# Transforms in plain float32 and an output projection placed among the long convolutions, in a two-block model kernel

## The chip, the cores and the metric

The kernel runs on one core of one Trainium2 chip. The metric is the time of one execution on the device, in microseconds (us), as the median of the runs shown. The engines are named as in the profile: PE is TensorE (PEld its weight loads), DVE is VectorE, ACT is ScalarE, POOL is GpSimd, SP is SyncE, which issues the DMAs.

## The reference, cut to what matters

Two blocks follow each other on a sequence of 512 positions and 1024 features. The change is in the mixing part of the first: a gated recurrence (branch a) and two long convolutions (branch b) read the same normalised input, and their projected outputs are gated and added. The rest of the first block is a mixture of 16 experts; the second block is two layers of attention and a feed-forward part.

```python
proj = h @ w_in[l]
a_x, a_gate, hy, gates = jnp.split(proj, ...)
xa = dwconv(a_x, conv_a_w[l], conv_a_b[l], ...)
h_a = rg_lru(xa, ..., False) + rg_lru(xa, ..., True)
y_a = (h_a * jax.nn.gelu(a_gate)) @ w_a_out[l]
hy = dwconv(hy, conv_b_w[l], conv_b_b[l], ...)
v, x1, x2 = jnp.split(hy, 3, axis=-1)
filt = hyena_filters(S, ...)
z = v
for n, gate in enumerate((x1, x2)):
    k = bidir_kernel(filt[:, n, 0], filt[:, n, 1])
    z = gate * fftconv(z, k, filt_bias[l, n])     # rfft, product, irfft
y_b = z @ w_b_out[l]
g_a, g_b = jnp.split(jax.nn.sigmoid(gates), 2, axis=-1)
x = x + (g_a * y_a + g_b * y_b) @ w_o[l]
```

## The kernel before

Activations lie with features on the 128 partitions and the 512 positions along a row: eight tiles of 128x512 make the 1024 features (`c.x`). A projection onto 128 output features (`proj`, line 952) takes a 128x1024 weight tile from HBM, splits it into a rounded float32r part and the rest (`split`, lines 152 and 155: a cast on ACT, a subtraction on DVE), and multiplies each of its eight 128x128 pieces with the two parts of an activation tile, which was split in the same way. `mm3` (lines 163 to 165) does this in three passes, hi x hi, hi x lo and lo x hi; 24 matmuls of 512 columns make one projection.

`body_t1` runs the stages of the first block's mixing part:

- **Norm and gelu gate** (lines 969 to 1009): eight projections whose gelu ends in `c.x`. `filter_mlp` (1073) loads the transform matrix, splits it into `dft_h` and `dft_l` (1075 to 1079) and makes the filters' hidden layer `HS`.
- **recurrence** (1112): the order is the string `STEPS_A`. A step `i` projects and convolves a tile of input, `r` runs the recurrence on it and multiplies the result into `c.x`, `f` makes a group of 256 filters (1253: a matmul, a product with the decay, a split into `sdh` and `sdl`), `t` transforms it (1291) and stores it in HBM (`c.kd`), `G` computes one of the 16 gate tiles (959) and stores it in HBM (`c.gates`).
- **branch_a** (1183): splits the eight tiles of `c.x` into `yah` and `yal`, then does eight projections with `w_a`; each loads its gate tile, forms (gate + 1) x result on DVE (1196) and stores it in HBM (`c.mg`).
- **branch_b** (1301): the order is the string `STEPS_B`. A step `c` projects and convolves one tile of v, x1 or x2 (24 in all; the digits are the group of 256 features, which of the three, and which half). `u` transposes a pair of tiles on PE into an operand of a transform (split into `uh`, `ul`, line 1335) or into a gate (1347). `L` is a long convolution (1364): forward transform, product with a stored filter spectrum (1354), combinations, a split into `Yh` and `Yl` (1385 to 1390). `M` is the inverse transform (1392) and the gating: `gated` (1404) makes the split operand of the second convolution, `last` (1417) transposes back and writes to `c.x`. `G` steps project the remaining six gates.
- **Merge** (1038 to 1069): splits `c.x`, projects with `w_b`, adds the tiles of `c.mg`, projects with `w_o`.

A transform is folded into products of 128x128 matrices with 256 columns (`part`, 1213, two products in one PSUM tile; `pair`, 1220, two such tiles whose sum and difference DVE forms). A filter transform has 12 products, a forward one 8, an inverse one 8. Each product is an `mm3`.

The strings set the order in which the steps are written. The framework then orders each engine's instructions by what is ready and earlier in the text, and adds the waits; in the timeline, matmuls of a transform stand between those of a projection. Tiles come from pools with a number of buffers for each name (`CFG1`: `U` 3, `cv` 9, `Y` 4 and so on), and a step waits where no buffer is free. PSUM gives three tiles to the projections, three to forward transforms and two to transposes and inverse transforms. All loads and stores are issued by SP, in one queue.

Of the kernel before, what the change touches and what calls it, by code (L numbers as in the profile page):

```python
# [844 lines left out]
STEPS_A = "i0 G8 i1 r0 f0 t0 i2 f2 r1 t2 f1 t1 i3 f3 r2 i4 G1 r3 i5 G0 r4 G2 i6 t3 r5 f4 t4 G4 f5 t5 f6 G7 i7 r6 t6 f7 G3 G5 r7 Gb t7 G6"  # L845
STEPS_B = "c000 c001 c020 c010 c120 c200 c011 u00 c100 c101 u01 L00 c201 M00 c110 u10 u20 c220 L01 c111 u11 L10 c021 c121 M01 M10 L11 c300 M11 c301 c320 L20 c210 c211 c321 c310 u21 u30 M20 c311 L21 L30 Gf u31 c221 M21 M30 Ga L31 M31 Ge Gc G9 Gd"
CFG1 = dict(acc=3, c=2, f=3, hA=0, lA=1, gh=0, gl=1, hB=0, lB=1, kh=0, kl=1, xh=0, xl=1, sh=0, sl=1, yh=0, yl=1, wl=1, rA=1, rX=1, bl=0, tA=5, tB=5, cv=9, U=3, Y=4, th=5, fA='vvvv', fB='vvvv', gB='vvvv', hB2='vvvv', xg=1, K=1, zh=0, zl=1)
ACTDVE, POOLDVE = ("act", "dve"), ("pool", "dve")
# [81 lines left out]
def body_t1(c, A):  # L930
# [86 lines left out]
    nc.vector.memset(quarter, 0.25)  # L1017
    dft_h = dp.tile([128, 2048], F32R, name="dft_h")
    dft_l = dp.tile([128, 2048], F32R, name="dft_l")
    HS = dp.tile([128, T], F32R, name="HS")  # L1020
    HS0 = dp.tile([128, 256], F32R, name="HS0")
    with pool("filt") as fp:
        softplus_cols(c, fp, sp, p1[:, 176:192], 16, -4.0)
        nc.vector.tensor_scalar(spd, sp, 2.0, None, op0=OP.mult)
        filter_mlp(c, A, fp, ps_f, dft_h, dft_l, HS, HS0)
    c.kd = c.dram.tile([8, 128, 4, T], F32, name="filters_dram")
    with pool("lru", 2, side="right") as lp:
        recurrence(c, A, h, proj, lp, ps_c, ps_f, hb, sp, spd, quarter, dft_h, dft_l, HS, HS0)
    with pool("lru2", 2, side="right") as lp:
        branch_a(c, A, h, proj, lp)  # L1030
    with pool("hy", 2, side="right") as bp:
        branch_b(c, A, h, proj, ps_c, ps_f, bp, dft_h, dft_l)
    d_ctx.close()
# [77 lines left out]

def recurrence(c, A, h, proj, lp, ps_c, ps_f, hb, sp, spd, quarter, dft_h, dft_l, HS, HS0):

# [5 lines left out]
    ws2 = WStream(c, lp, 2, 2, size=T, tag="l")  # L1119
    filters = make_filters(c, A, ps_f, t, lp, ws2, dft_h, dft_l, HS, HS0)  # L1120

# [60 lines left out]

def branch_a(c, A, h, proj, lp):

    nc, mg = c.nc, c.mg
    ys = []
    for y in c.x:
        hi, lo = lp.tile([128, T], F32R, name="yah", bufs=8), lp.tile([128, T], F32R, name="yal", bufs=8)
        split(c, y, hi, lo)
        ys.append((hi, lo))  # L1190
    for m in range(8):
        g = lp.tile([128, T], F32, name="ga", bufs=4)
        nc.sync.dma_start(g, c.gates[m])
        ps = proj(A["w_a"][m], ys)
        o = lp.tile([128, T], F32, name="gy")
        nc.vector.scalar_tensor_tensor(o, g, 1.0, ps, op0=OP.add, op1=OP.mult)
        nc.sync.dma_start(mg[m], o)
# [8 lines left out]

def make_transform(c, ps_f, t, dft_h, dft_l, NT, st2):
    nc = c.nc

    def transform(cosv, sinv, out):  # L1210


        def part(r, mats=(0, 1)):
            ps = ps_f.tile([128, T], F32, name="fps", tag="f")
            for half, v in enumerate((cosv, sinv)):
                s = slice((2 * r + mats[half]) * 128, (2 * r + mats[half] + 1) * 128)
                mm3(nc, ps[:, half * Q:(half + 1) * Q], (dft_h[:, s], dft_l[:, s]), (v[0][:, r], v[1][:, r]), True, True)
            return ps
# [28 lines left out]

def make_filters(c, A, ps_f, t, bp, ws, dft_h, dft_l, HS, HS0):
    nc = c.nc
    NT = CFG1["tA"]  # L1250
    transform = make_transform(c, ps_f, t, dft_h, dft_l, NT, CFG1["fA"])

    def filters(n, q):
# [9 lines left out]
        nc.sync.dma_start(br, A["f_bias"][n:n + 1, q * Q:(q + 1) * Q])  # L1263
        sh, sl = t("sdh", 1, F32R, 8 * Q), t("sdl", 1, F32R, 8 * Q)
        r = lambda a: a.rearrange("p (g i n) -> p g i n", g=2, i=4)
        for i in range(4):
            ps = ps_f.tile([128, T], F32, name="fps", tag="f")
            if i:
                nc.tensor.matmul(ps, HS[:, i * 128:(i + 1) * 128], wh, start=True, stop=False)
                nc.tensor.matmul(ps, HS[:, i * 128:(i + 1) * 128], wl, start=False, stop=True)  # L1270
            else:


                for g in range(2):
                    o = ps[:, g * Q:(g + 1) * Q]
                    for k, (H, at) in enumerate(((HS0[:, :128], g), (HS0[:, 128:], 1 - g))):
                        for j, w in enumerate((wh, wl)):
                            nc.tensor.matmul(o, H, w[:, at * Q:(at + 1) * Q], start=k + j == 0, stop=k + j == 2)
            fb = t("fb", NT, tag="tmp")
            d = t("dec", 2, n=Q)  # L1280
            nc.sync.dma_start(d, A["decay"][q][:, i * Q:(i + 1) * Q])
            nc.vector.tensor_tensor(fb.rearrange("p (g n) -> p g n", g=2), ps.rearrange("p (g n) -> p g n", g=2),
                                    d[:, None, :].to_broadcast([128, 2, Q]), op=OP.mult)
            if i == 0:
                o = fb[0:1].rearrange("p (g n) -> p g n", g=2)
                nc.vector.scalar_tensor_tensor(o, br[:, None, :].to_broadcast([1, 2, Q]), 1.0 / 512.0, o, op0=OP.mult, op1=OP.add)
# [13 lines left out]

def branch_b(c, A, h, proj, ps_c, ps_f, bp, dft_h, dft_l):

# [29 lines left out]
    def operand():  # L1332
        return [t(nm, 2, F32R, 4 * Q) for nm in ("uh", "ul")]

    def to_operand(tiles):

        hi, lo = [blocks(a) for a in operand()]

        def put(src, j):
            s = slice(j * 128, (j + 1) * 128)  # L1340
            nc.scalar.copy(hi[:, :, s], src)
            nc.vector.tensor_tensor(lo[:, :, s], src, hi[:, :, s].bitcast(F32), op=OP.subtract)
# [21 lines left out]
    def long_conv(u, K):  # L1364
# [472 lines left out]
```

## Time and profile before

| | |
|---|---|
| median of 3 runs | 3002.57 us (3001.47 to 3002.89) |
| the profiled execution's own time | 2998.99 us |
| its span in the profile | 2997.2 us |
| mean granted PE clock | 0.976 of full speed |
| norm and gelu gate | 0 to 64 us |
| recurrence and filters | 64 to 268 us |
| branch_a | 268 to 317 us |
| branch_b | 317 to 604 us |
| merge | 604 to 710 us |
| experts | 710 to 1651 us |
| second block | 1651 to 2997 us |

The stages' limits were read from the first and last instructions that write their tiles, and rounded. In the profile, "busy" is the time in which at least one instruction of an engine runs; matmuls overlap, so their work is better read from the distance of their starts. A row of the timeline has the start, the duration, engine, line, operation, output<-inputs, shape and count; an `x8` row is eight instructions in a row. The granted clock is the share of its full clock that PE was given. A row of a wait names who waited, for whom, the sum in us, how often, and the longest.

### The profile page before, as it was taken

To read this page: it belongs to the slowest core of one execution; us is meant where nothing else is said; L and a number is where in the kernel's file an instruction comes from. 1 tells how busy PE (TensorE), PEld (TensorE's weight loads), DVE (VectorE), ACT (ScalarE), POOL (GpSimd) and SP (SyncE) were. 2 spreads that over 40 slices of the span, in tenths; PEclk is the share of its full clock that TensorE was granted. 3 is DMA by queue.
4 is the path that set the end of the run, shared out by engine and by line. 5 is a ranking of instruction groups with operands and counts; after the bars stand their busy time and mean duration, and the time that the engine had idled before them with its cause. 6 is when DMAs were issued, how large, how long until landed. Compare 5 with 4: busy or idle time off the path is not lost.

```text
span 2997.2 us, 35639 instructions
## 1 busy us (share of the span) xinstructions
PE 2789.5 (93%) x13524; PEld 1851.5 (62%) x13524; DVE 1595.7 (53%) x3205; ACT 966.0 (32%) x1629; POOL 177.6 (6%) x150
## 2 busy tenths in 40 slices
PE   8898988699999999998988899899999999999998
PEld 7677876575333333333333676688888776688887
DVE  7997599954122222222211889663435788654345
ACT  6774333231000000000000358442223367433224
POOL 0000000000000000000000223200000233100000
PEclk9999998899999999999999899999999999999999
DMA  4344322258999999999999233232222323232324
GB/s 158 130 141 165 120 95 75 98 199 353 417 421 420 420 421 421 421 421 421 420 421 392 89 94 86 64 105 98 94 96 97 119 76 83 76 103 94 99 92 134
DMA packets 136356, 617.94 MB, mean 206 GB/s; under 512 B 17423, under 2 KB 31575, under 8 KB 84600
## 3 DMA queue, kind: packets, MB, share of 16 engines
q1 hardware_dynamic: 136184, 615.65, 54.4%
q8 instruction: 107, 1.75, 0.2%
q14 instruction: 65, 0.53, 0.1%
HBM read 582.03 MB, written 16.78 MB: 200 GB/s over the span
## 4 chain that ended last, share of the span: by engine, by line
PE 64%; DMA 12%; DVE 9%; issue 4%; ACT 1%; POOL 1%; SPq 0%; DVEq 0%; ACTq 0%; POOLq 0%
DMA ew<-experts 12%; PE acc L165 9%; PE acc L164 9%; PE acc L163 9%; PE gps L1684 8%; PE dps L1709 4%; PE S L163 4%; PE S L164 4%; PE S L165 4%; PE o L615 2%; PE acc L1736 2%; PE S L549 2%; PE tp L598 1%; PE acc L1637 1%; DVE wl L155 1%
## 5 line engine op out<-in xcount | busy, mean ns | idle before, releaser
L152 ACT CAST wh<-wr 128x1024 fp32r<-128x1024 f32 (+3 forms) x294 | 291.5, 992 | 793.5 <-PE acc L164 503.4
L1684 PE MATMUL gps<-ew,xe 128*64 128x512 f32 x2048 | 488.8, 597 | 8.8 <-DMA ew<-experts 8.8
L155 DVE TENSOR_TENSOR wl<-wr,wh 128x1024 fp32r<-128x1024 f32 (+3 forms) x291 | 336.2, 1157 | 66.6 <-ACT wh L152 65.7
L1684 PEld LDWEIGHTS gps<-ew,xe 128*64 128x64 f32 x2048 | 151.0, 137 | 285.4 <-issue 253.7
L165 PE MATMUL acc<-hh,wl 128*128 128x512 f32 x768 | 307.1, 401 | 18.0 <-DVE wl L155 17.9
L163 PE MATMUL acc<-hh,wh 128*128 128x512 f32 x768 | 312.2, 406 | 7.2 <-DVE x L1317 3.0
L164 PE MATMUL acc<-hl,wh 128*128 128x512 f32 x768 | 308.6, 402 | 0.0
L1709 PE MATMUL dps<-ew,hT 128*64 128x512 f32 x992 | 224.9, 600 | 15.2 <-DMA ew<-experts 8.8
L164 PE MATMUL acc<-fl,wh 128*128 128x512 f32 (+1 forms) x576 | 213.4, 371 | 0.0
L165 PE MATMUL acc<-fh,wl 128*128 128x512 f32 (+1 forms) x576 | 213.2, 370 | 0.0
L163 PE MATMUL acc<-fh,wh 128*128 128x512 f32 (+1 forms) x576 | 212.9, 370 | 0.0
L165 PE MATMUL S<-hh,wl 128*128 128x512 f32 x512 | 199.9, 391 | 0.0
L164 PE MATMUL S<-hl,wh 128*128 128x512 f32 x512 | 198.9, 389 | 0.0
L163 PE MATMUL S<-hh,wh 128*128 128x512 f32 x512 | 198.9, 389 | 0.0
L1692 DVE TENSOR_TENSOR g<-g,gps 128x512 f32<-128x512 f32 x32 | 21.9, 685 | 330.8 <-PE gps L1684 322.1
L165 PEld LDWEIGHTS acc<-hh,wl 128*128 128x128 f32 x768 | 147.4, 192 | 52.9 <-DVE wl L155 22.3
L163 PEld LDWEIGHTS acc<-hh,wh 128*128 128x128 f32 x768 | 148.0, 193 | 44.8 <-issue 9.4
L1709 PEld LDWEIGHTS dps<-ew,hT 128*64 128x64 f32 x992 | 75.0, 138 | 156.0 <-issue 128.4
L164 PEld LDWEIGHTS acc<-hl,wh 128*128 128x128 f32 x768 | 147.8, 192 | 31.2 <-issue 4.2
L1691 ACT ACTIVATE g<-gps 128x512 f32<-128x512 f32 x32 | 19.2, 599 | 365.7 <-PE gps L1684 353.2
L395 DVE TENSOR_TENSOR x<-acc,x 128x512 f32<-128x512 f32 x56 | 38.8, 692 | 184.1 <-PE acc L165 184.1
L379 DVE SCALAR_TENSOR_TENSOR r<-S,rsb 128x512 f32<-128x512 f32 x64 | 44.1, 692 | 162.4 <-PE S L165 158.7
(422 smaller groups left out, 4740.8 us busy)
## 6 DMA issues: line engine op xcount, KB each, us to landing
ew<-experts SPq DMA_DIRECT2D x384, 1024.0 KB, 19.8
wr<-w_down SPq DMA_DIRECT2D x72, 512.0 KB, 3.3
wr<-w_up SPq DMA_DIRECT2D x64, 512.0 KB, 3.3
wr<-w_in SPq DMA_DIRECT2D x56, 512.0 KB, 3.6
wr<-in_w SPq DMA_DIRECT2D x38, 512.0 KB, 3.4
R<-qkc SPq DMA_DIRECT2D x72, 128.0 KB, 2.3
filters_dram<-K SPq DMA_DIRECT2D x8, 1024.0 KB, 4.5
K<-filters_dram SPq DMA_DIRECT2D x8, 1024.0 KB, 5.0
```

The costliest lines, as they stand in the source:

```text
L152: nc.scalar.copy(hi, src)
L155: (nc.vector if lo_eng == "dve" else nc.gpsimd).tensor_tensor(lo, src, hi.bitcast(F32), op=OP.subtract)
L163: nc.tensor.matmul(ps, W[0], X[0], start=start, stop=False)
L164: nc.tensor.matmul(ps, W[0], X[1], start=False, stop=False)
L165: nc.tensor.matmul(ps, W[1], X[0], start=False, stop=stop)
L379: nc.vector.scalar_tensor_tensor(r, ps, 0.0, rsb, op0=OP.max, op1=OP.mult)
L395: nc.vector.tensor_tensor(x[m], ps, x[m], op=OP.add)
L549: nc.tensor.matmul(ps, q[:, qs], k[:, ks], start=a == 0, stop=a == len(passes) - 1)
L615: nc.tensor.matmul(o[s * 64:(s + 1) * 64, q], v[:, j, vc[s]:vc[s] + 64], pts[s][:, a], start=a == 0, stop=a == len(js) - 1)
L1684: nc.tensor.matmul(ps[h * 64:(h + 1) * 64], xes[e][:, kt], W[:, k, h * T:(h + 1) * T], start=kt == 0, stop=kt == 7)
L1709: nc.tensor.matmul(outs[e][col * 64:(col + 1) * 64], hT[:, j, p * 64:(p + 1) * 64], W[:, p, h * T:(h + 1) * T], start=cc == 0 and j == 0 a ...
L1736: nc.tensor.matmul(ps, Y[f // 4][j][:, (f % 4) * 128:(f % 4 + 1) * 128], st[f // 4], start=j == 0, stop=j == n - 1)
```

## The change

Two things change.

First, the transforms. The matrix is kept as loaded, one float32 tile `dft`, and each product is one plain float32 matmul where `mm3` was. No operand of a transform is split any more: the filters' `sdh`/`sdl`, the convolutions' `uh`/`ul` and `Yh`/`Yl` become single float32 tiles (`fs`, `u`, and the tile `Z` itself), written directly by the instruction that fed the split. `HS` and `HS0` move to a pool that is closed after the recurrence.

Second, branch_a as a stage goes. Its work becomes steps of `STEPS_B`: `y0` to `y3` split two tiles of `c.x` each, `A0` to `A7` do one projection with its gate. The gate's tile takes its buffer from the two of the tag `gate`, and the result is written over it. The first `A` stands behind 20 of the 24 `c` steps.

Buffers: `U` 4 for 3, `cv` 8 for 9, `u` 2 in place of two each of `uh` and `ul`, `fs` 2 in place of one each of `sdh` and `sdl`; `Yh` and `Yl` go.

```diff
-STEPS_B = "c000 c001 c020 c010 c120 c200 c011 u00 c100 c101 u01 L00 c201 M00 c110 u10 u20 c220 L01 c111 u11 L10 c021 c121 M01 M10 L11 c300 M11 c301 c320 L20 c210 c211 c321 c310 u21 u30 M20 c311 L21 L30 Gf u31 c221 M21 M30 Ga L31 M31 Ge Gc G9 Gd"
+STEPS_B = "c000 c001 c020 c010 c120 c200 c011 u00 c100 c101 u01 L00 y0 c201 M00 c110 u10 u20 c220 L01 c111 u11 y1 L10 c021 c121 M01 M10 y2 L11 c300 M11 c301 c320 L20 y3 c210 c211 A0 c321 c310 u21 u30 A1 M20 c311 A2 L21 A3 L30 A4 Gf u31 c221 M21 A5 M30 Ga A6 L31 A7 M31 Ge Gc G9 Gd"
...
-    raw = fp.tile([128, 2048], F32, name="dft_raw")
-    nc.sync.dma_start(raw, A["dft"])
-    for j in range(4):
-        split(c, raw[:, j * T:(j + 1) * T], dft_h[:, j * T:(j + 1) * T], dft_l[:, j * T:(j + 1) * T])
+    nc.sync.dma_start(dft, A["dft"])
...
-def branch_a(c, A, h, proj, lp):
...
 def make_transform
-                mm3(nc, ps[:, half * Q:(half + 1) * Q], (dft_h[:, s], dft_l[:, s]), (v[0][:, r], v[1][:, r]), True, True)
+                nc.tensor.matmul(ps[:, half * Q:(half + 1) * Q], dft[:, s], v[:, r], start=True, stop=True)
...
 def filters
-            nc.vector.tensor_tensor(fb.rearrange("p (g n) -> p g n", g=2), ps.rearrange("p (g n) -> p g n", g=2),
+            nc.vector.tensor_tensor(fs[:, :, i], ps.rearrange("p (g n) -> p g n", g=2),
                                     d[:, None, :].to_broadcast([128, 2, Q]), op=OP.mult)
...
-            split(c, s3, r(sh)[:, :, i], r(sl)[:, :, i], hi_eng=ACTDVE[CFG1["sh"]], lo_eng=POOLDVE[CFG1["sl"]])
...
 def to_operand
-            nc.scalar.copy(hi[:, :, s], src)
-            nc.vector.tensor_tensor(lo[:, :, s], src, hi[:, :, s].bitcast(F32), op=OP.subtract)
+        by_time(tiles, lambda src, j: nc.scalar.copy(u[:, :, j * 128:(j + 1) * 128], src))
...
 def long_conv
-            split(c, Z[:, r * T:(r + 1) * T], hi, lo, hi_eng=ACTDVE[CFG1["yh"]], lo_eng=POOLDVE[CFG1["yl"]])
+        return Z.rearrange("p (r n) -> p r n", r=4)
...
 def inverse
-                    mm3(nc, o, (dft_h[:, w], dft_l[:, w]), (Y[r][0][:, s], Y[r][1][:, s]), half == 0, half == 1)
+                    nc.tensor.matmul(o, dft[:, w], Y[:, r, s], start=half == 0, stop=half == 1)
...
 def gated
-            z = t("z1", NT, tag="tmp")
-            nc.vector.tensor_tensor(blocks(z), ps, g[:, s], op=OP.mult)
-            split(c, blocks(z), hi[:, s], lo[:, s], hi_eng=ACTDVE[CFG1["zh"]], lo_eng=POOLDVE[CFG1["zl"]])
+            nc.vector.tensor_tensor(u[:, s], ps, g[:, s], op=OP.mult)
...
+    ya = []
+
+    def parts(q):
+        for y in c.x[2 * q:2 * q + 2]:
+            hi, lo = bp.tile([128, T], F32R, name="yah", bufs=8), bp.tile([128, T], F32R, name="yal", bufs=8)
+            split(c, y, hi, lo)
+            ya.append((hi, lo))
+
+    def out_a(m):
+        g = t("ga", 2, tag="gate")
+        nc.sync.dma_start(g, c.gates[m])
+        ps = proj(A["w_a"][m], ya)
+        nc.vector.scalar_tensor_tensor(g, g, 1.0, ps, op0=OP.add, op1=OP.mult)
+        nc.sync.dma_start(c.mg[m], g)
```

More of the change, by code (lines that the diff above doesn't have):

```diff
@@ L845 @@
 STEPS_A = "i0 G8 i1 r0 f0 t0 i2 f2 r1 t2 f1 t1 i3 f3 r2 i4 G1 r3 i5 G0 r4 G2 i6 t3 r5 f4 t4 G4 f5 t5 f6 G7 i7 r6 t6 f7 G3 G5 r7 Gb t7 G6"
-STEPS_B = "c000 c001 c020 c010 c120 c200 c011 u00 c100 c101 u01 L00 c201 M00 c110 u10 u20 c220 L01 c111 u11 L10 c021 c121 M01 M10 L11 c300 M11 c301 c320 L20 c210 c211 c321 c310 u21 u30 M20 c311 L21 L30 Gf u31 c221 M21 M30 Ga L31 M31 Ge Gc G9 Gd"
-CFG1 = dict(acc=3, c=2, f=3, hA=0, lA=1, gh=0, gl=1, hB=0, lB=1, kh=0, kl=1, xh=0, xl=1, sh=0, sl=1, yh=0, yl=1, wl=1, rA=1, rX=1, bl=0, tA=5, tB=5, cv=9, U=3, Y=4, th=5, fA='vvvv', fB='vvvv', gB='vvvv', hB2='vvvv', xg=1, K=1, zh=0, zl=1)
+STEPS_B = "c000 c001 c020 c010 c120 c200 c011 u00 c100 c101 u01 L00 y0 c201 M00 c110 u10 u20 c220 L01 c111 u11 y1 L10 c021 c121 M01 M10 y2 L11 c300 M11 c301 c320 L20 y3 c210 c211 A0 c321 c310 u21 u30 A1 M20 c311 A2 L21 A3 L30 A4 Gf u31 c221 M21 A5 M30 Ga A6 L31 A7 M31 Ge Gc G9 Gd"
+CFG1 = dict(acc=3, c=2, f=3, hA=0, lA=1, gh=0, gl=1, hB=0, lB=1, kh=0, kl=1, xh=0, xl=1, wl=1, rA=1, rX=1, bl=0, tA=5, tB=5, cv=8, U=4, u=2, th=5, fA='vvvv', fB='vvvv', gB='vvvv', hB2='vvvv', xg=1, K=1)
 ACTDVE, POOLDVE = ("act", "dve"), ("pool", "dve")
@@ L1017, in body_t1 @@
     nc.vector.memset(quarter, 0.25)
[L1018 to L1021, printed above, removed]
+    dft = dp.tile([128, 2048], F32, name="dft")
+    hs_ctx = ExitStack()
+    hsp = hs_ctx.enter_context(pool("hs", side="right"))
+    HS = hsp.tile([128, T], F32R, name="HS")
+    HS0 = hsp.tile([128, 256], F32R, name="HS0")
     with pool("filt") as fp:
@@ L1024, in body_t1 @@
         nc.vector.tensor_scalar(spd, sp, 2.0, None, op0=OP.mult)
-        filter_mlp(c, A, fp, ps_f, dft_h, dft_l, HS, HS0)
+        filter_mlp(c, A, fp, ps_f, dft, HS, HS0)
     c.kd = c.dram.tile([8, 128, 4, T], F32, name="filters_dram")
     with pool("lru", 2, side="right") as lp:
-        recurrence(c, A, h, proj, lp, ps_c, ps_f, hb, sp, spd, quarter, dft_h, dft_l, HS, HS0)
-    with pool("lru2", 2, side="right") as lp:
-        branch_a(c, A, h, proj, lp)
+        recurrence(c, A, h, proj, lp, ps_c, ps_f, hb, sp, spd, quarter, dft, HS, HS0)
+    hs_ctx.close()
     with pool("hy", 2, side="right") as bp:
-        branch_b(c, A, h, proj, ps_c, ps_f, bp, dft_h, dft_l)
+        branch_b(c, A, h, proj, ps_c, ps_f, bp, dft)
     d_ctx.close()
@@ L1070, in body_t1, with filter_mlp @@
     w_ctx.close()
-def filter_mlp(c, A, fp, ps_f, dft_h, dft_l, HS, HS0):
+def filter_mlp(c, A, fp, ps_f, dft, HS, HS0):
     nc = c.nc
     p1 = c.p1
-    raw = fp.tile([128, 2048], F32, name="dft_raw")
-    nc.sync.dma_start(raw, A["dft"])
-    for j in range(4):
-        split(c, raw[:, j * T:(j + 1) * T], dft_h[:, j * T:(j + 1) * T], dft_l[:, j * T:(j + 1) * T])
+    nc.sync.dma_start(dft, A["dft"])
     z = fp.tile([33, T], F32, name="z")
@@ L1109, in filter_mlp, with recurrence @@
         nc.vector.tensor_scalar(HS0[:, k:k + 1], HS[:, 0:1].bitcast(F32), 0.5, None, op0=OP.mult)
-def recurrence(c, A, h, proj, lp, ps_c, ps_f, hb, sp, spd, quarter, dft_h, dft_l, HS, HS0):
+def recurrence(c, A, h, proj, lp, ps_c, ps_f, hb, sp, spd, quarter, dft, HS, HS0):
     nc, p1 = c.nc, c.p1
@@ L1119, in recurrence @@
     ws2 = WStream(c, lp, 2, 2, size=T, tag="l")
-    filters = make_filters(c, A, ps_f, t, lp, ws2, dft_h, dft_l, HS, HS0)
+    filters = make_filters(c, A, ps_f, t, lp, ws2, dft, HS, HS0)
     def inputs(ct):
@@ L1180, in recurrence @@
             c.gate(n, lp, hi_eng=ACTDVE[CFG1["gh"]], lo_eng=POOLDVE[CFG1["gl"]])
-def branch_a(c, A, h, proj, lp):
[L1185 to L1197, printed above, removed]
 Q = 256
@@ L1204, in blocks, with make_transform @@
     return a.rearrange("p (b n) -> p b n", n=Q)
-def make_transform(c, ps_f, t, dft_h, dft_l, NT, st2):
+def make_transform(c, ps_f, t, dft, NT, st2):
     nc = c.nc
@@ L1245, in make_transform, with make_filters @@
     return transform
-def make_filters(c, A, ps_f, t, bp, ws, dft_h, dft_l, HS, HS0):
+def make_filters(c, A, ps_f, t, bp, ws, dft, HS, HS0):
     nc = c.nc
     NT = CFG1["tA"]
-    transform = make_transform(c, ps_f, t, dft_h, dft_l, NT, CFG1["fA"])
+    transform = make_transform(c, ps_f, t, dft, NT, CFG1["fA"])
     def filters(n, q):
@@ L1263, in filters @@
         nc.sync.dma_start(br, A["f_bias"][n:n + 1, q * Q:(q + 1) * Q])
-        sh, sl = t("sdh", 1, F32R, 8 * Q), t("sdl", 1, F32R, 8 * Q)
-        r = lambda a: a.rearrange("p (g i n) -> p g i n", g=2, i=4)
+        fs = t("fs", 2, n=8 * Q).rearrange("p (g i n) -> p g i n", g=2, i=4)
         for i in range(4):
@@ L1278, in filters @@
                             nc.tensor.matmul(o, H, w[:, at * Q:(at + 1) * Q], start=k + j == 0, stop=k + j == 2)
-            fb = t("fb", NT, tag="tmp")
             d = t("dec", 2, n=Q)
             nc.sync.dma_start(d, A["decay"][q][:, i * Q:(i + 1) * Q])
-            nc.vector.tensor_tensor(fb.rearrange("p (g n) -> p g n", g=2), ps.rearrange("p (g n) -> p g n", g=2),
+            nc.vector.tensor_tensor(fs[:, :, i], ps.rearrange("p (g n) -> p g n", g=2),
                                     d[:, None, :].to_broadcast([128, 2, Q]), op=OP.mult)
             if i == 0:
-                o = fb[0:1].rearrange("p (g n) -> p g n", g=2)
+                o = fs[0:1, :, 0]
                 nc.vector.scalar_tensor_tensor(o, br[:, None, :].to_broadcast([1, 2, Q]), 1.0 / 512.0, o, op0=OP.mult, op1=OP.add)
-            s3 = fb.rearrange("p (g n) -> p g n", g=2)
-            split(c, s3, r(sh)[:, :, i], r(sl)[:, :, i], hi_eng=ACTDVE[CFG1["sh"]], lo_eng=POOLDVE[CFG1["sl"]])
-        return r(sh), r(sl)
+        return fs
     def transforms(n, q, fs):
-        sh, sl = fs
         kt = t("K", 1, n=4 * T)
-        transform((sh[:, 0], sl[:, 0]), (sh[:, 1], sl[:, 1]), kt)
+        transform(fs[:, 0], fs[:, 1], kt)
         nc.sync.dma_start(c.kd[4 * n + q].rearrange("p a b -> p (a b)"), kt)
@@ L1298, in make_filters, with branch_b @@
     return filters
-def branch_b(c, A, h, proj, ps_c, ps_f, bp, dft_h, dft_l):
+def branch_b(c, A, h, proj, ps_c, ps_f, bp, dft):
     nc, p1 = c.nc, c.p1
@@ L1332, in operand @@
     def operand():
-        return [t(nm, 2, F32R, 4 * Q) for nm in ("uh", "ul")]
+        return blocks(t("u", CFG1["u"], n=4 * Q))
     def to_operand(tiles):
-        hi, lo = [blocks(a) for a in operand()]
-        def put(src, j):
-            s = slice(j * 128, (j + 1) * 128)
-            nc.scalar.copy(hi[:, :, s], src)
-            nc.vector.tensor_tensor(lo[:, :, s], src, hi[:, :, s].bitcast(F32), op=OP.subtract)
-        by_time(tiles, put)
-        return hi, lo
+        u = operand()
+        by_time(tiles, lambda src, j: nc.scalar.copy(u[:, :, j * 128:(j + 1) * 128], src))
+        return u
     def to_gate(tiles):
@@ L1350, in to_gate @@
         return g
-    transform = make_transform(c, ps_f, t, dft_h, dft_l, NT, CFG1["fB"])
+    transform = make_transform(c, ps_f, t, dft, NT, CFG1["fB"])
     def cmul(u, k):
@@ L1384, in long_conv @@
         e[3].tensor_tensor(o[:, 2:8:5], b0, b1, op=OP.add)
-        out = []
-        for r in (0, 2, 1, 3):
-            hi, lo = t("Yh", CFG1["Y"], F32R), t("Yl", CFG1["Y"], F32R)
-            split(c, Z[:, r * T:(r + 1) * T], hi, lo, hi_eng=ACTDVE[CFG1["yh"]], lo_eng=POOLDVE[CFG1["yl"]])
-            out.append((hi, lo))
-        return [out[i] for i in (0, 2, 1, 3)]
+        return Z.rearrange("p (r n) -> p r n", r=4)
     def inverse(Y, put):
@@ L1400, in inverse @@
                     s = slice(half * Q, (half + 1) * Q)
-                    mm3(nc, o, (dft_h[:, w], dft_l[:, w]), (Y[r][0][:, s], Y[r][1][:, s]), half == 0, half == 1)
+                    nc.tensor.matmul(o, dft[:, w], Y[:, r, s], start=half == 0, stop=half == 1)
             put(ps.rearrange("p (i n) -> p i n", i=2), h)
     def gated(Y, g):
-        hi, lo = [blocks(a) for a in operand()]
+        u = operand()
         def put(ps, h):
             s = slice(2 * h, 2 * h + 2)
-            z = t("z1", NT, tag="tmp")
-            nc.vector.tensor_tensor(blocks(z), ps, g[:, s], op=OP.mult)
-            split(c, blocks(z), hi[:, s], lo[:, s], hi_eng=ACTDVE[CFG1["zh"]], lo_eng=POOLDVE[CFG1["zl"]])
+            nc.vector.tensor_tensor(u[:, s], ps, g[:, s], op=OP.mult)
         inverse(Y, put)
-        return hi, lo
+        return u
     def last(Y, gates, dst):
@@ L1430, in kernel_of @@
         return k.rearrange("p (a b) -> p a b", a=4)
+    ya = []
[10 more added lines that the diff above has]
+        nc.sync.dma_start(c.mg[m], g)
     cv, us, ys = {}, {}, {}
     for s in STEPS_B.split():
+        if s[0] in "yA":
+            (parts if s[0] == "y" else out_a)(int(s[1]))
+            continue
         if s[0] == "G":
```

## The prediction

> **What bounds the kernel now.** I read the page first, then busy time by stage, then what TensorE waits for, then single rows of the timeline for prices. The page says that TensorE (PE) bounds the whole:
>
> ```profile
> span 2997.2 us, 35639 instructions
> PE 2789.5 (93%) x13524; PEld 1851.5 (62%) x13524; DVE 1595.7 (53%) x3205; ACT 966.0 (32%) x1629; POOL 177.6 (6%) x150
> ```
>
> An average of 93% hides stages with other limits, and the change touches the first 604 us only. The table of stretches (length, then busy us of PE, PEld, DVE, ACT, POOL, then granted clock, DMA share, GB/s) divides them:
>
> ```profile
> 0.00:64.00 64.00, 56.46 (x231) 43.73 (x232) 51.96 (x117) 39.55 (x56) 0.45 (x5) 1.00 0.46 160
> 64.00:268.00 204.00, 184.74 (x905) 149.22 (x903) 191.37 (x309) 147.21 (x207) 0.00 (x0) 0.95 0.39 133
> 268.00:317.00 49.00, 47.58 (x197) 38.82 (x198) 20.49 (x26) 12.39 (x16) 0.00 (x0) 0.93 0.57 193
> 317.00:370.00 53.00, 53.00 (x253) 44.56 (x252) 26.43 (x31) 18.01 (x23) 0.00 (x0) 1.00 0.35 119
> 370.00:604.00 234.00, 183.56 (x939) 152.10 (x937) 218.81 (x306) 76.29 (x117) 0.26 (x2) 0.88 0.26 87
> 710.00:1651.00 941.00, 865.95 (x4147) 326.79 (x4148) 207.19 (x694) 61.16 (x103) 14.28 (x33) 0.99 1.00 416
> ```
>
> 64 to 268 is the recurrence with the filters, 268 to 317 the output projection of the gated branch (branch_a), 317 to 604 the long convolutions (branch_b), 710 to 1651 the experts. In the recurrence VectorE (DVE) is the limit, 191 of 204. In branch_a PE is full and DVE has little to do. In branch_b the first 53 us are PE alone, and the other 234 are DVE, 219 busy, while PE has holes and a lower clock:
>
> ```profile
> 420.00:445.00 25.00, 16.01 (x71) 12.58 (x70) 25.00 (x37) 6.59 (x10) 0.00 (x0) 0.81 0.22 74
> 495.00:520.00 25.00, 13.72 (x63) 10.61 (x62) 23.14 (x33) 6.08 (x11) 0.00 (x0) 0.66 0.25 84
> 570.00:604.00 34.00, 13.81 (x74) 12.27 (x74) 25.75 (x36) 5.47 (x10) 0.00 (x0) 0.67 0.00 0
> ```
>
> The waits of PE between 317 and 604 (us in total, times, longest) show what it lacks there: a split operand of the inverse transform (Yh), a split weight (wl), both made behind DVE's queue.
>
> ```profile
> PE cps L163 <- ACT Yh L152: 17.0, 2, 16.2
> PE acc L165 <- DVE wl L155: 15.9, 2, 8.3
> ```
>
> So two neighbouring stages, one PE-full and one DVE-full, are laid over each other, and DVE loses the transforms' splits. The experts run at a DMA share of 1.00: if what is ahead ends earlier, their loads start earlier, and the gain is kept.
>
> **Price of a product.** Before, a 128x256 product of a transform is three passes (mm3). Starts in the timeline give their spacing, and that of a wider plain float32 product:
>
> ```profile
> 487.00 0.28 PE L163 MATMUL cps<-Yh,dft_h 128*128 128x256 f32 x1
> ...
> 489.25 0.28 PE L165 MATMUL cps<-Yh,dft_l 128*128 128x256 f32 x1
> ...
> 653.10 0.39 PE L164 MATMUL acc<-ml,wh 128*128 128x512 f32 x1
> ...
> 658.32 0.39 PE L163 MATMUL acc<-mh,wh 128*128 128x512 f32 x1
> ...
> 353.98 1.12 PE L1329 MATMUL cps<-ident,v 128*128 128x128 f32 x8
> 354.85 0.47 PE L163 MATMUL acc<-hh,wh 128*128 128x512 f32 x1
> ...
> 838.65 7.13 PE L1736 MATMUL acc<-st,Y 128*128 128x512 f32 x16 [0.79 <-ACT Y L1728]
> ...
> L1736 PE MATMUL acc<-st,Y x112: 592/592/697, 838.6 to 1542.9; 128*128 128x512 f32 x112
> ```
>
> From 487.00 to 489.25 are 20 split passes of 256 columns, 19 steps of 0.118 us; from 653.10 to 658.32 are 24 of 512 columns, 23 steps of 0.227. So mm3 costs 0.354. L1736 issues 8 plain products there and the trace has 16 records: a plain product is two records, (7.13 - 0.59) / 15 = 0.436 apart, 0.592 being one record's duration, so 0.87 at 512 columns. No row shows 256. From below it is half, 0.436; from above 0.87, if narrower operands bring nothing. I take 0.436, since split passes halve with the columns, and a transpose with a 128x128 load of its own follows the last after 0.87 / 8 = 0.109. So PE pays **0.082 more** per product. The code has 12 products in each of 8 filter transforms (96), and 8 forward and 8 inverse in each of 8 long convolutions (128).
>
> Going from split passes to plain ones and back has a price too:
>
> ```profile
> 658.63 1.03 PE L1550 MATMUL lps<-x,first 128*16 128x512 f32 x2
> 659.60 0.50 PE L164 MATMUL acc<-ml,wh 128*128 128x512 f32 x1
> 659.93 0.39 PE L165 MATMUL acc<-mh,wl 128*128 128x512 f32 x1
> ```
>
> From 658.32 (above) to 659.93 are 1.61 us for one split pass, two plain records and one split pass, 0.227 + 0.87 + 0.227 = 1.33: **a visit costs 0.28**. The transforms stand among projections in PE's stream; one visit per PSUM tile would make 96 of them, one per pair of tiles 48; I take 72, half in each stage, 10 us each.
>
> **Recurrence.** The rows for the splits (xcount | busy us, mean ns):
>
> ```profile
> L155 DVE TENSOR_TENSOR sdl<-fb,sdh 128x512 fp32r<-128x512 f32 x32 | 20.8, 677 | 0.1
> L155 DVE TENSOR_TENSOR Yl<-U,Yh 128x512 fp32r<-128x512 f32 x32 | 20.0, 685 | 0.0
> L155 DVE TENSOR_TENSOR ul<-z,uh 128x512 fp32r<-128x512 f32 x8 | 5.4, 688 | 1.5 <-ACT uh L152 1.4
> L1342 DVE TENSOR_TENSOR ul<-cps,uh 128x512 fp32r<-128x512 f32 x8 | 5.3, 688 | 0.1
> L155 DVE TENSOR_TENSOR wl<-wr,wh 128x1024 fp32r<-128x1024 f32 x39 | 47.6, 1222 | 29.7 <-ACT wh L152 29.6
> L1196 DVE SCALAR_TENSOR_TENSOR gy<-ga,acc 128x512 f32<-128x512 f32 x8 | 5.5, 688 | 27.1 <-PE acc L165 27.1
> ```
>
> DVE goes from 191.4 to 170.6. PE's work at the full clock is now 288 transform passes x 0.118 = 34, 64 filter passes of 256 columns 7.5, the other 905 - 352 = 553 x 0.227 = 125.5: 167. After it is 167 + 96 x 0.082 + 10 = 185, so **PE becomes the longer engine**. The stage now stands 12.6 over its longest; I keep that: 185 + 12.6 = 197.6, 6 less. From -18 (no visits and little overhead) to +4 (two engines at over 85% in each other's way).
>
> **Branch_a and branch_b together (268 to 604, 336 us).** DVE: 20.5 + 26.4 + 218.8 = 265.7, less 20.0 + 5.4 + 5.3 = 235. The eight moved projections keep all that they issue: a weight split (1.22) and the gating (0.69) each, the eight splits of x in pairs, their loads and stores on SP's queue. PE: 317 to 604 has 1192 records, 384 transform passes at 0.118 (45), 96 transposes at 0.109 (10.5), 712 others at 0.227 (162), 217 in all; the moved projections are 8 x 24 x 0.227 = 43.6; 128 x 0.082 = 10.5; visits 10. Sum 281. The opening 53 us stay as they are, full of PE, DVE 26. There remain 228 for PE and 209 for DVE, where it was 234 with 219 on DVE, 15 over the longest. 228 + 15 + 53 = 296: **40 less**. What hides the 43.6 us of moved PE work are the holes shown above; without that cover they cost what they do now. Bounds: -60 (no overhead, no visits), -15 (overhead of 40, as when the last chains of DVE work stand alone again).
>
> Added waits: the store of a gated tile on SP holds back the weight loads queued behind it.
>
> ```profile
> SPq L228 <- DVE wl L155: 162.5, 30, 19.6
> SPq L1197 <- DVE gy L1196: 3.6, 1, 3.6
> ```
>
> SP's weight loads wait for a free buffer anyway, 162 us in all, and the store waited 3.6 once: nothing taken, at most 4. The gate tiles share two buffers with the projections' gates; nothing, as DVE frees them after 0.69. One conv buffer less and one U more are about even, 0 to 3 either way. Last, the splits of the transform matrix in the first stage go, four of 512 columns like the sdl rows (0.68). DVE is 52 of 64 there, so 0 is taken, 3 at most. ScalarE's half of every split goes as well; it is never a limit (147 of 204 at most), so nothing for it.
>
> **Sum:** -6 - 40 = -46. The profiled run took 2998.99 which is 3.6 below the median of 3002.57 and 1.8 over its span; taken off the median: **2956**. A difference of 0.2% (6 us) is about what a measurement of this kernel can tell.
>
> **Rivals.**
> (a) The moved steps come too late. The first stands after 20 of the 24 convolution tiles, so the holes at 420 and 495 may stay, and only the last, at 570, fills: 20 idle us there, and some 7 as the clock rises from 0.67. Of the moved 43.6 then 17 stay uncovered, and what DVE gives back is taken by the plain products and visits (20): 287 + 17 + 20 = 324 for 336, and with the recurrence 18 less: 2985. For it: PE is full between those holes, so what stands behind them can't close them unless its operands are ready early. Against: the splits of x are ready from the start, and DVE, the cause of the holes, gets 31 lighter.
> (b) More than forecast: with PE fed, the clock stays at 1.00 and the overhead goes to a third in both stages, 18 less: 2938.
> (c) Slower: the load of a plain pass isn't hidden behind only 256 columns. The load's own duration (ns, min/median/max) is:
>
> ```profile
> L1736 PEld LDWEIGHTS acc<-st,Y x112: 186/190/190, 838.6 to 1542.5; 128*128 128x128 f32 x112
> ```
>
> Then a product is 2 x (0.218 + 0.190) = 0.816, 0.462 over mm3. Recurrence: 167 + 44 + 10 + 12.6 = 234, +30. The rest: 217 + 43.6 + 59 + 10 + 15 = 345, +9. 3042. It decides from about 0.64 us per product, where 224 times the excess has eaten the 46. Against: L1550's records, which load 16 columns, are 1.03 - 0.59 = 0.44 apart, no less than L1736's 0.436 with 128 columns, so at 512 the load is hidden; and transposes load 128 columns every 0.109. The Trainium skill, TensorE: Matmul & The Clock Gate (Part 3, The mechanism) says that a weight load overlaps running matmuls only when their row groups differ. By that rule this rival would hold; the trace disagrees at 512 columns, by the 0.44 and 0.436, and no run here shows 256. The same page of the Trainium skill (Weight-path perf modes) says that the fast weight load is off for float32, which speaks against plain products; its formula for a load (LDWEIGHTS, columns over 1.2 per ns) gives 107 ns, and by that estimate, exposed twice, the sum would end near 3004.
>
> **Chances.** Forecast 0.62 (alone 2940 to 2970), (a) 0.19, (b) 0.10, (c) 0.06, about even 0.03. The range holds the forecast, (a) and part of (b): 2933 to 2987. Faster 0.90, within 0.2% 0.03, slower 0.07.
>
> **What would show it.** Right: plain transform records 0.21 to 0.22 apart, two per product, 448 in all; no sdl, Yl, ul; the stage ahead of the merge ends near 558 instead of 604, granted clock near 1 and PE over 90% busy in branch_b; the recurrence near 198. Wrong: records 0.3 or more apart; a stretch of PE below 60% with DVE full ahead of the first moved projection, which is (a); a recurrence longer than 208; experts' time that isn't shifted by what the earlier stages gain.

## The result, and the profile after

The changed kernel took 2953.06 us (median of 4 runs, 2948.47 to 2957.56), the kernel before 3002.73 beside it (4 runs, 3001.47 to 3003.65): a ratio of 0.9836, 95% interval 0.9823 to 0.9848. That is 1.6% faster, and 3 us from the forecast of 2956. The profiled execution took 2954.03, with a span of 2952.2.

The page's first lines after (span; busy us, share and instructions of each engine):

```profile
span 2952.2 us, 35034 instructions
PE 2791.5 (95%) x13300; PEld 1847.5 (63%) x13300; DVE 1545.0 (52%) x3121; ACT 922.0 (31%) x1553; POOL 177.6 (6%) x150
```

PE is busy as long as before (2789.5 us) in a span that is 45 shorter; what went away is idle time. The table of stretches (length, then busy us of PE, PEld, DVE, ACT, POOL, then granted clock, DMA share, GB/s) shows the recurrence, the joint stage of long convolutions and output projection, four pieces of that stage, and the experts:

```profile
64.00:266.00 202.00, 191.16 (x831) 151.77 (x830) 174.59 (x280) 130.11 (x175) 0.00 (x0) 0.97 0.40 133
266.00:557.00 291.00, 278.52 (x1250) 229.13 (x1248) 235.23 (x313) 84.27 (x116) 0.26 (x2) 0.98 0.35 119
360.00:380.00 20.00, 14.13 (x64) 11.54 (x62) 20.00 (x30) 4.51 (x6) 0.00 (x0) 0.92 0.28 98
420.00:440.00 20.00, 15.90 (x71) 12.41 (x70) 19.82 (x27) 5.05 (x8) 0.00 (x0) 0.91 0.24 84
470.00:510.00 40.00, 40.00 (x183) 33.52 (x182) 39.31 (x54) 9.94 (x14) 0.00 (x0) 1.00 0.43 146
510.00:557.00 47.00, 46.09 (x211) 37.38 (x209) 33.74 (x46) 11.71 (x16) 0.26 (x2) 1.00 0.38 132
663.00:1604.00 941.00, 866.64 (x4147) 326.72 (x4146) 207.35 (x690) 60.61 (x102) 14.32 (x33) 0.99 1.00 415
```

Before, the last 234 us of branch_b had PE at 184 busy and a clock of 0.88. Now PE has 278.5 of 291 at 0.98, and the end, where PE had 13.8 of 34, is full. Two small holes are left, in the pieces from 360 and from 420, both with DVE full: the old pattern, further ahead. The experts last 941 us as before.

The transforms' products by form (xcount | busy us, mean ns | idle before) and, in the timeline, two visits of plain products among split passes:

```profile
L1197 PE MATMUL fps<-fs,dft 128*128 128x256 f32 x192 | 49.7, 394 | 4.0 <-DVE fs L1260 2.8 <-ACT so L1203 0.7 <-DVE so L1208 0.5
L1197 PE MATMUL fps<-u,dft 128*128 128x256 f32 x128 | 30.4, 383 | 0.0
L1365 PE MATMUL cps<-U,dft 128*128 128x256 f32 x128 | 29.3, 382 | 0.0
```

```profile
83.42 0.40 PE L165 MATMUL acc<-hh,wl 128*128 128x512 f32 x1
83.66 1.03 PE L1197 MATMUL fps<-fs,dft 128*128 128x256 f32 x4
84.33 0.58 PE L163 MATMUL acc<-hh,wh 128*128 128x512 f32 x1
84.75 0.40 PE L164 MATMUL acc<-hl,wh 128*128 128x512 f32 x1
...
495.83 0.40 PE L165 MATMUL acc<-hh,wl 128*128 128x512 f32 x1
496.07 3.62 PE L1365 MATMUL cps<-U,dft 128*128 128x256 f32 x16
499.34 0.58 PE L163 MATMUL acc<-yah,wh 128*128 128x512 f32 x1
499.76 0.39 PE L164 MATMUL acc<-yal,wh 128*128 128x512 f32 x1
```

There are 448 records, two per product. One record lasts 0.38 (the mean of the third form), so the 16 records in 3.62 us are (3.62 - 0.38) / 15 = 0.216 apart: a product costs 0.432. From start to start, 83.42 to 84.75 are 1.33 us for two split passes and four plain records, 2 x 0.227 + 4 x 0.216 = 1.318; from 495.83 to 499.76 are 3.93 for 2 x 0.227 + 16 x 0.216 = 3.91. These visits cost 0.01 and 0.02 us, not 0.28. They are typical, not uniform: 29 visits between 64 and 700 us stand directly between split passes of 512 columns, with no wait; worked out in the same way, 22 of them cost 0.02 or less, the other seven 0.05 to 0.20, and all together 1.05 us.

What PE lacked between 266 and 558 (us in total, times, longest), and the two places in the timeline where it lacked it (in brackets the idle time ahead):

```profile
PE acc L165 <- DVE wl L155: 10.6, 2, 7.0
PE acc L163 <- ACT wh L152: 0.5, 1, 0.5
```

```profile
381.09 0.80 PE L165 MATMUL acc<-hh,wl 128*128 128x512 f32 x1 [6.96 <-DVE wl L155]
...
434.71 0.80 PE L165 MATMUL acc<-hh,wl 128*128 128x512 f32 x1 [3.63 <-DVE wl L155]
```

The 17.0 us in which PE waited for Yh are gone with Yh, and the 15.9 for split weights are 10.6, all of it at the two holes.

In the following table of starts (us), taken from the trace of each kernel run, the joint stage begins with its first matmul, of branch_a in before and plain_only and of a convolution in the others, and ends with the first split of the merge; the experts' column has the first and the last matmul of their first layer (`gps`):

| kernel | joint stage from | merge from | length | experts' first and last `gps` | span |
|---|---|---|---|---|---|
| before | 268.4 | 604.4 | 336.0 | 722.6, 1634.5 | 2997.2 |
| after | 262.5 | 557.3 | 294.8 | 673.9, 1586.5 | 2952.2 |
| plain_only | 263.9 | 578.6 | 314.7 | 699.6, 1612.6 | 2973.7 |
| split_load | 277.5 | 584.3 | 306.8 | 703.9, 1616.8 | 2978.6 |
| filters_mm3 | 263.5 | 557.7 | 294.2 | 674.7, 1587.6 | 2949.3 |
| a_early | 259.2 | 548.0 | 288.8 | 669.1, 1581.3 | 2944.1 |
| double_b | 262.6 | 598.1 | 335.5 | 716.8, 1629.7 | 2994.9 |
| a_last | 261.7 | 558.4 | 296.7 | 675.4, 1588.7 | 2950.1 |
| u_first | 261.5 | 551.3 | 289.8 | 669.9, 1582.8 | 2947.9 |

The merge begins 47.1 earlier, 5.9 from the recurrence and 41.2 from the joint stage. The experts carry 48 on, and the second block gives 3 back. Its first stretch, before and then after:

```profile
1651.00:1800.00 149.00, 136.79 (x674) 101.74 (x673) 125.01 (x240) 66.75 (x124) 39.86 (x25) 0.94 0.30 93
```

```profile
1603.00:1755.00 152.00, 139.95 (x676) 103.85 (x674) 125.51 (x241) 66.98 (x125) 39.87 (x25) 0.92 0.30 91
```

The same work took 152 us instead of 149 at a clock of 0.92 instead of 0.94. The change need not be the cause: by the last two columns of the table, the time from the last `gps` to the end is 1362.7 before, 1361.1 in plain_only, 1362.8 in a_early and 1365.7 in after, so single traces differ that much whatever the kernel. Five of the kernels above have the code of after in the recurrence (a_early, double_b, a_last, u_first and after itself) and start the joint stage between 259.2 and 262.6, so differences of some 3 us in that column are no finding.

### The profile page after: what moved, and what is told of

Its sections match the earlier page's. It is cut to its first block, busy times and chain, and to the rows that moved or that the text cites. A ratio compares the mean times of both kernels' runs of the same rounds, so it can differ in the third digit from the quotient of the medians.

```text
span 2952.2 us, 35034 instructions
## 1 busy us (share of the span) xinstructions
PE 2791.5 (95%) x13300; PEld 1847.5 (63%) x13300; DVE 1545.0 (52%) x3121; ACT 922.0 (31%) x1553; POOL 177.6 (6%) x150
## 4 chain that ended last, share of the span: by engine, by line
PE 76%; DVE 10%; DMA 7%; issue 4%; ACT 2%; POOL 1%; SPq 0%; DVEq 0%; ACTq 0%; POOLq 0%
PE gps L1665 11%; PE acc L165 10%; PE acc L164 10%; PE acc L163 10%; PE dps L1690 6%; DMA ew<-experts 5%; PE S L163 4%; PE S L164 4%; PE S L165 4%; PE o L615 2%; PE fps L1197 2%; PE acc L1618 2%; PE acc L1717 2%; PE S L549 2%; PE tp L598 1%
```

## Experiments

The theory: two halves add up. Plain products take the splits from DVE, which was the limit of branch_b, and the moved projections give PE work for the holes; the joint stage is then PE's. The rivals were that one half alone does it, that the place of the moved steps decides, or that another wait does. The kernel before took 3001.58 beside the first four kernels (7 runs) and 3001.47 beside the others (13 runs).

**1. One half alone (plain_only).** branch_a stays a stage; only the products are plain:

```
-STEPS_B = "... L00 y0 c201 ... A0 ... A7 M31 ..."
+STEPS_B of before
+    with pool("lru2", 2, side="right") as lp:
+        branch_a(c, A, h, proj, lp)
```

> Only the transforms are changed to plain float32 products; the projection of the gated branch stays a stage of its own. Theory (a PE-full and a DVE-full stage are laid over each other, and DVE is relieved): the recurrence 5 less as in the changed kernel; the long convolutions have 214 us of DVE and 229 of PE, the opening 53 with 26 of DVE, so 188 of DVE and 15 of overhead behind it: 256 where it was 287. In all some 36 less than before, about 2967, DVE still the longer engine behind the opening. Rival 1 (the move is the gain, plain products only make room for it): at most 10 less, 2993. Rival 2 (DVE's relief is the whole gain): 47 less, 2956, no different from the changed kernel.

2975.71 us, ratio 0.9916 (0.99 to 0.9931): 26 faster. Its stretches (recurrence, branch_a, branch_b):

```profile
64.00:264.00 200.00, 189.07 (x819) 149.71 (x818) 175.29 (x282) 130.79 (x177) 0.00 (x0) 0.97 0.40 133
264.00:312.00 48.00, 45.91 (x190) 37.19 (x191) 18.38 (x23) 10.85 (x14) 0.00 (x0) 0.93 0.57 190
312.00:579.00 267.00, 241.13 (x1072) 197.37 (x1072) 217.19 (x289) 73.76 (x102) 0.26 (x2) 0.95 0.29 100
```

That lies between the theory's 2967 and the 2993 of the rival of little gain. The next stage begins at 263.9, 4.5 earlier than before. Branch_b goes from 288 to 266 us, not further, and PE idles 26 in it. In branch_a DVE is 18 of 48 busy, and that slack can't be used while the stages follow each other. At the merge, plain products alone bring 25.8 of the 47.1, and the move another 21.3. The move by itself, with split products, wasn't tried: by the sizes and buffers in the code, its tiles would take 136 kB per partition in that stage, where those of the changed kernel take 118. Whether they would fit isn't shown; what the move brings without plain products stays open.

**2. The splits' load given back (split_load).** For each removed split DVE does an operation of the same size in place, 32 in the recurrence and 48 in the joint stage; results are unchanged:

```
+            nc.vector.tensor_tensor(fs[:, :, i], fs[:, :, i], fs[:, :, i], op=OP.max)
...
+            nc.vector.tensor_tensor(z, z, z, op=OP.max)
```

> The changed kernel with DVE's part of every removed split put back as an instruction of the same size on the same tile, in place (maximum of a tile with itself, which keeps its values), 32 among the filters and 48 in the long convolutions. Theory: DVE 266 in the joint stage, 29 of it in the opening 51, so 237 and 15 behind it: 303 where it is 290, and the recurrence loses its 5: some 18 over the changed kernel, 2971. Rival 2 (DVE's relief is the whole gain): all 47 lost, 3000. Rival 3 (PE alone bounds the joint stage, the move is the whole gain): within 4 of the changed kernel, 2953 to 2957.

2978.44 us, ratio 0.9923 (0.9907 to 0.994), 25 over after: nearer to the theory's 2971 than to either rival. Recurrence and joint stage:

```profile
64.00:277.00 213.00, 192.81 (x818) 151.85 (x817) 193.27 (x312) 129.03 (x173) 0.00 (x0) 0.96 0.38 127
277.00:584.00 307.00, 285.76 (x1268) 233.28 (x1266) 264.55 (x362) 85.73 (x118) 0.26 (x2) 0.97 0.34 114
```

In the joint stage 29 us of DVE work cost 12.0, near the 13 expected. In the recurrence 21 us cost 15, three times the 5 expected: PE and DVE are both busy for 193, and the stage takes 20 more than either. Why it takes so much more than in filters_mm3 (experiment 3), where DVE is as busy, isn't shown.

**3. The filters' transforms as split passes again (filters_mm3).** In the recurrence the transforms keep their splits and three passes, for which half of the matrix is split again in the first stage; the long convolutions stay plain:

```
+            s3 = fb.rearrange("p (g n) -> p g n", g=2)
+            split(c, s3, r(sh)[:, :, i], r(sl)[:, :, i], hi_eng="act", lo_eng="dve")
...
+        transform((sh[:, 0], sl[:, 0]), (sh[:, 1], sl[:, 1]), kt)
```

> The changed kernel with the filters' transforms as three split passes with split operands, as before; the long convolutions plain. Theory (the recurrence gained about 5 because DVE was its limit): 5 over the changed kernel, 2958. Rival (PE is the longer engine there since the change, so the plain products cost what they give): within 2 of the changed kernel or up to 8 faster.

2953.89 us, ratio 0.9848 (0.9828 to 0.9868): no different from after, as the rival had it. The recurrence:

```profile
64.00:266.00 202.00, 186.60 (x924) 150.54 (x923) 191.51 (x310) 148.74 (x208) 0.00 (x0) 0.97 0.40 135
```

DVE has its 191.5 us of before, PE its 187 (185 before), and the joint stage begins at 263.5, as with plain products (262.5). So in the new order plain products bring the recurrence nothing that can be measured: 21 off DVE is paid with 7 to 8 on PE (96 x 0.078).

In the old order they do bring something. plain_only has them too, begins its next stage with the splits of `c.x` as the kernel before does, and is 4.5 earlier. DVE's last operation on a filter and the first matmul of the next stage, before and then in plain_only, and that operation of DVE in this kernel:

```profile
267.74 0.68 DVE L1243 TENSOR_TENSOR K<-so 128x512 f32<-128x512 f32 x1
268.37 0.80 PE L163 MATMUL acc<-yah,wh 128*128 128x512 f32 x1 [3.10 <-ACT yah L152]
...
262.06 0.68 DVE L1242 TENSOR_TENSOR K<-so 128x512 f32<-128x512 f32 x1
263.87 0.50 PE L163 MATMUL acc<-yah,wh 128*128 128x512 f32 x1 [1.91 <-ACT yah L152]
...
266.78 0.69 DVE L1231 TENSOR_TENSOR K<-so 128x512 f32<-128x512 f32 x1
```

In before and plain_only PE idles until ACT has cast the first tile of `c.x`. In this kernel DVE ends its filters almost as late as before, but the next stage begins 3.3 ahead of that operation, since its first steps are convolutions of `h`. So either part, less DVE work or a stage that begins with convolutions, brings 4.5 to 4.9, and both together 5.9. Each start is from one trace, and the order at that boundary was not varied by itself.

**4. The moved steps earlier (a_early).** Splits of `c.x` ahead of `L00`, `A0` to `A7` spread from `L00` to `M21`:

```
STEPS_B = "... u01 y0 y1 y2 y3 L00 A0 c201 M00 c110 u10 u20 A1 c220 L01 c111 u11 A2 L10 c021 c121 M01 M10 A3 L11 c300 M11 A4 c301 c320 L20 c210 c211 A5 c321 c310 u21 u30 M20 c311 L21 A6 L30 Gf u31 c221 M21 A7 M30 ..."
```

> The changed kernel with the moved steps spread from the first long convolution on: the four y steps ahead of L00, A0 behind L00, then A1 to A4 before c301, A5 to A7 behind. Theory: the holes that PE still has between 370 and 470 (11 us idle of 100) fill, and as PE is the longer engine the joint stage comes 5 to 10 nearer to its 271 us of PE work: 2943 to 2948. Rival (early fill delays the convolution tiles that the chain of DVE work needs, and the end stands alone again): 5 to 20 slower than the changed kernel.

2948.21 us, ratio 0.9823 (0.9807 to 0.984). The whole joint stage and its two early pieces:

```profile
259.00:548.00 289.00, 280.32 (x1260) 230.87 (x1258) 236.32 (x314) 86.06 (x119) 0.26 (x2) 0.99 0.37 126
360.00:380.00 20.00, 20.00 (x92) 16.81 (x92) 19.93 (x30) 6.16 (x8) 0.00 (x0) 1.00 0.39 128
380.00:400.00 20.00, 16.84 (x70) 13.02 (x69) 19.40 (x25) 2.02 (x3) 0.00 (x0) 0.91 0.35 124
```

The hole at 360 is closed, a smaller one follows at 380, and the stage takes 288.8 instead of 294.8. Its median is the lowest of all, 5 below that of after, but the two ratios' intervals overlap, so the times don't show a gain over after. The stage's 6 us are read from one trace each; u_first (experiment 7), whose `A` steps stand at nearly the same places, has 289.8.

**5. More load on PE (double_b).** The plain products of the long convolutions are doubled in number, 128 x 0.43 = 55 us more PE work. Each forward product is issued twice, as shown; in an inverse transform the first product of each pair is issued three times, which adds as many:

```
+                if cosv is sinv:
+                    nc.tensor.matmul(o, dft[:, s], v[:, r], start=True, stop=True)
                 nc.tensor.matmul(o, dft[:, s], v[:, r], start=True, stop=True)
```

> The changed kernel with every plain product of the long convolutions issued twice (the first result is written over by the second), 128 more products of 0.43: 55 us more for PE, nothing more for DVE. Theory (PE is the longer engine of the joint stage, 271 of 295, and has few holes left): the stage grows by 35 to 55, 2988 to 3008. Rival (DVE and the chains still set the end, PE has room): by less than 25, under 2978.

2993.78 us, ratio 0.9973 (0.9962 to 0.9983). The joint stage:

```profile
263.00:598.00 335.00, 331.87 (x1519) 277.59 (x1517) 237.72 (x315) 85.84 (x118) 0.26 (x2) 1.00 0.31 106
```

It grows by 40.7 of the 55, as the theory had it. 12.5 us idle of PE become 3.1, the clock goes to 1.00, and the rest is length. PE is the longer engine of the joint stage, with some 14 us to spare.

**6. The moved steps last (a_last).** `A0` to `A7` stand behind `M31`, the last inverse transform:

```
STEPS_B = "... M30 Ga L31 M31 A0 A1 A2 A3 A4 A5 A6 A7 Ge Gc G9 Gd"
```

> The changed kernel with A0 to A7 written behind M31, ahead of the last four gates. Theory: projections run nearly in the order written, so the holes between 370 and 470 stay open or are filled by other steps too soon, and the end fills: 5 to 15 slower than the changed kernel, 2958 to 2968. Rival (each engine takes what is ready, the place in the text doesn't matter): within 3 of the changed kernel.

2954.09 us, ratio 0.9847 (0.9832 to 0.9861): the theory's 5 to 15 slower did not come, and it is within 3 of after, as the rival had it. Three pieces of its joint stage:

```profile
360.00:400.00 40.00, 32.98 (x141) 26.58 (x139) 37.72 (x52) 8.29 (x12) 0.00 (x0) 0.91 0.33 109
400.00:440.00 40.00, 34.57 (x151) 27.73 (x150) 39.43 (x53) 11.57 (x17) 0.00 (x0) 0.91 0.24 79
520.00:557.00 37.00, 37.00 (x167) 30.23 (x166) 16.33 (x22) 8.54 (x12) 0.26 (x2) 1.00 0.48 158
```

The holes ahead are as in after, the end is full. In the trace the eight projections don't come last: their matmuls run from 478.5 to 535.4, around the products of `M31` at 525, where in after they run from 415.9 to 529.6. What the moved steps have to fill is the end, where the last convolutions hang on DVE; for that, both places behind the first hole did equally well, and only a place ahead of it (a_early) shortened the stage further.

**7. The first convolution's operands first (u_first).** As a_early, with `u00`, `u01` and `L00` ahead of all but four of the convolution tiles:

```
STEPS_B = "c000 c001 u00 c010 c011 u01 L00 c020 c120 c200 y0 y1 y2 y3 c100 c101 A0 ..."
```

> The order of a_early with the first pair's transposes and long convolution written sooner: u00 behind two convolution tiles, L00 behind four. Theory: DVE's work starts some 25 us sooner, in the opening where PE is full and DVE half idle; what is left behind for DVE is smaller and PE's holes with it: the joint stage 3 to 12 shorter than in a_early, 2936 to 2946. Rival (PE bounds the joint stage, 271 of 289 in a_early, and what is over it are the last chain and cold stretches): within 3 of a_early.

2949.74 us, ratio 0.9836 (0.982 to 0.9853); the joint stage takes 289.8 against 288.8 of a_early, so the theory's 3 to 12 shorter fell, and the rival's reading stands: with PE at 280 of 289 in a_early, an earlier start of DVE's chain has little left to fill.

**8. What makes a visit dear (router_wide).** The row that gave 0.28 loads a narrow operand of 16 columns (the experts' scores, `lps`). Here it has 128, the others of no use:

```
-        nc.tensor.matmul(self.lps[:16], self.wr[:, k], x[k], ...)
+        nc.tensor.matmul(self.lps, self.first[:, 16*k:16*k+128], x[k], ...)
```

> The changed kernel with the router's product (lps) padded by zero columns from 16 to 128 output columns. It is the product from which a price of 0.28 to 0.30 for a visit of plain products among split passes was read; the trace of the changed kernel has visits of the transforms at 0.00 to 0.05. Theory (the price belongs to the narrow output, not to float32): the spacing around lps falls to that of the passes alone, 1.31 from the last split pass ahead to the second behind, no time of note. Rival (it belongs to a product that reads x or a new PSUM tile): 1.61 as before.

2954.3 us in a single run. One of its visits in the timeline:

```profile
610.82 0.39 PE L163 MATMUL acc<-mh,wh 128*128 128x512 f32 x1
611.08 1.12 PE L1533 MATMUL lps<-x,first 128*128 128x512 f32 x2
611.64 0.79 PE L164 MATMUL acc<-ml,wh 128*128 128x512 f32 x1
612.27 0.40 PE L165 MATMUL acc<-mh,wl 128*128 128x512 f32 x1
```

From 610.82 to 612.27 are 1.45 us, where before and after have 1.61: with work of 1.33, 0.12 of 0.28 is left. The seven visits that stand between split passes agree within 0.005 in each of the three traces. That lies between the theory (nothing left) and the rival (all of it): more than half of the price belongs to the narrow operand. What the rest belongs to stays open; most of the transforms' visits pay none of it.

## Why the prediction was right, and where it wasn't

**Plain product, 0.436:** right, 0.432 measured, two records each of half the 512-column spacing. Rival (c), a load exposed behind 256 columns, falls with it: it needed over 0.64. By the Trainium skill, TensorE: Matmul & The Clock Gate (Part 3, The mechanism), a load overlaps running matmuls only when their row groups differ. These loads fill all 128 rows and last 0.19 by their own records, and the 0.216 between matmul records disagrees at 256 columns too.

**Visits, 20 us:** wrong. The step that failed is the transfer of one row's price to another shape: 1.61 us around a 16-column operand said 0.28, the transforms pay 0.01 to 0.02 in most of theirs, and over half of the price went when the operand was widened. At the mean of the 29 visits (0.036), 72 cost about 3 us, not 20.

**Overhead, 12.6 and 15:** too low, by about as much as the visits were too high. For the joint stage the sum was 281 of PE work with 15 over it. Without visits it is 271, and the stage took 294.8: 24 over. Of these about 12 are idle time (278.5 busy of 291), and some 6 go with the clock of 0.98 (271 / 0.98 = 277). The last 6 stay open. Two wrong terms cancelled, so that the stage's -40 came out as -41.2 is in part luck.

**Recurrence, -6:** the number was met (-5.9), the reason only in part. The prediction took 20.8 us off DVE and made PE the longer engine, and it is (191 of 202, DVE 175). With the old order of the stages that brings 4.5 (plain_only). But filters_mm3, which undoes just that and keeps the new order, begins the next stage as early within 1 us. The sum had no term for the boundary, where the next stage no longer begins with splits of `c.x` behind the last filter work; either part alone gives most of the 5.9, so in the changed kernel the gain can't be put down to DVE's relief.

**Cover for the moved projections:** right. 43.6 us of PE work was added to the long convolutions, and the two stages together still shrank. The gain comes about half from each part: DVE's relief alone (plain_only) gave 22 us in branch_b, and laying the stages over each other 21 more.

**Rival (a), steps too late:** partly there. Its mechanism exists: one hole stays ahead of the first moved projection, whose matmuls begin at 415.9, one follows 19 us behind that, and a_early closes one of them for 6 us. It was priced at 29 over the forecast, and the holes were worth 11 us of waits. a_last points to why: what the moved steps must fill is the end. **Rival (b)**, a third of the overhead, fell: the overhead rose.

**The store on SP, 0 to 4:** the wait was mis-sized. SP in the joint stage, after and then a_early:

```profile
SPq L1410 <- DVE ga L1409: 43.0, 8, 15.9
```

```profile
SPq L1410 <- DVE ga L1409: 56.5, 8, 12.8
```

It waits 43 us for gated tiles, not 4. As a_early waits 56.5 and has the shorter stage, the time in this row isn't a cost by itself; what the queue cost wasn't measured, and PE waits only 11 us in all in that stage of after.

**First stage, 0:** the last gelu projection's last matmul starts 1.5 us later than before (58.4 for 56.9), although four splits left the stage; in the other kernels it is 58.5 to 59.6. Counted from there the recurrence is 7.4 shorter, and the -5.9 holds both. No run tells the cause. **Experts:** right, DMA share 1.00 in 941 us both times, and what came ahead was carried through, less the 3 of the second block.

## What to carry to other kernels

Where one engine fills a stage and another fills the next, look at merging the two in one order as well as at making either faster: here nearly half of the gain at the merge came with the overlap, and the place of the moved steps mattered little as long as they filled the end. Take the price of an instruction from a row of the same operand shape, and don't carry a switching cost from a narrow operand to a wide one. A term that comes out right can have a second cause that the sum left out; it took two runs that each undo one part (filters_mm3 and plain_only) to see that either part gives most of the gain.

## What the runs showed of the hardware

A plain float32 product with 256 columns is two records 0.216 us apart, with a fresh 128x128 load for each that lasts 0.19; in 22 of 29 visits between split passes of 512 columns it costs 0.02 or less to switch, in the others up to 0.20. A visit with a 16-column operand costs 0.28, the same with 128 columns 0.12. In the recurrence, two engines at 193 us each took 213 together (split_load), while one at 191 and the other at 175 to 187 took 202 (after, filters_mm3).
